# Attention on one core: the product of softmax weights and values issued as four matmuls of 32 queries

## The chip, the core and the metric

The kernel runs on one core of a Trainium2 chip. Its time is the device time of one execution, in microseconds (us). Five engines work side by side and meet through semaphores: TensorE (PE in the profile; its weight loads have a row of their own, PEld), VectorE (DVE), ScalarE (ACT), GpSimd (POOL) and SyncE (SP), which issues most of the DMA transfers. A matmul on TensorE has a stationary operand, which a weight load puts into the 128 x 128 array, and a moving operand, whose columns are streamed through it; the result goes to PSUM, one partition for each column of the stationary operand. Where an instruction uses 32 columns of the array only, the profile writes its shape as 128\*32 in place of 128\*128.

## The reference, cut to what matters

One layer of a hybrid decoder, for a prompt of 2048 tokens and a decode step of 8 samples. The part that the change touches is the dilated attention of the prompt: 6 heads of 64, each evaluated in three branches of (window, dilation).

```python
DILATED_BRANCHES = ((128, 1), (512, 4), (2048, 16))
...
def dilated_prompt(q, k, v, rel_bias, window, dil):
    ...                       # queries regrouped by residue mod dil, in blocks of 128
    s = jnp.einsum('bnqrhe,bnkrhe->bnrhqk', qb, kc).astype(jnp.float32) * scale + bias
    s = jnp.where(mask[None, :, None, None], s, NEG)
    lse = jax.nn.logsumexp(s, axis=-1)
    p = jnp.exp(s - lse[..., None]).astype(v.dtype)
    o = jnp.einsum('bnrhqk,bnkrhe->bnqrhe', p, vc).reshape(B, s_pad, H, E)[:, :S]
```

Each block of 128 queries meets its own block of 128 keys and, where there is one, the block before it. The second einsum, weights times values, is the product in question. Behind attention come an mLSTM mixer, an output projection and an MLP of width 4096, all in float32.

## The kernel before, in words

The work runs in stages: normalisation and the projections of the values; the projections of keys and queries; the projections of the mLSTM's inputs (`pmm` in the profile), the second half of them interleaved with attention; the mLSTM (`ppq`, `psA`, `up`, `nu`), interleaved with the rest of attention; the output projection; the MLP (`pf`), which takes the larger half of the time.

Attention is a generator. It goes through 6 heads, three branches and, in each branch, four groups of four blocks of 128 queries. Two blocks at a time go through three steps. `front` makes the scores: for each block two matmuls into the PSUM tile `ps_s` (L1073), then VectorE adds the bias and takes the row minimum (L1075), and ScalarE the exponential (`ex`, L1077). `turn` transposes the 128 x 128 pieces of `ex` on TensorE into `pt` (L1086), and VectorE copies them to SBUF as `pT` (L1088). `weigh` multiplies them by the values: for each block of queries and each of its one or two blocks of keys, one matmul with `pT` (128 keys x 128 queries) as the stationary operand and 65 columns of values and ones (`V`, 64 + 1) as the moving one, into a slice of the PSUM tile `po` (L1101). Two key blocks are added up in PSUM by the flags `start` and `stop`. After four blocks of queries ScalarE copies `po` to `R4` (L1103), and SyncE writes it to DRAM. There is one buffer of `po`; `ps_s` and `pt` share a pool that the other stages use too.

There are 450 such products: per head 16 in the branch with dilation 16 (one key block each), 28 in that with dilation 4 and 31 in that with dilation 1. All operands are float32, and each float32 matmul stands in the trace as two records of load and matmul, so that L1101 has 900 records.

The generators set the order in which instructions are written. A scheduler then orders them on each engine, by its own estimate of when each is ready; on TensorE it mixes the products with scores, transposes, projections and the mLSTM's matmuls. The instructions of one engine run in the order so fixed. In the mLSTM the state update has four matmuls of the form that the change uses (L441): 32 columns of the stationary operand each, written to 32 partitions each, with 161 moving columns.

Of the kernel before, what the change touches and what calls it, by code (L numbers as in the profile page):

```python
# [16 lines left out]
P = 128  # L17
# [42 lines left out]
def body(tc, I, O):  # L60
# [18 lines left out]
    pe = nc.tensor  # L79
# [959 lines left out]
    def attention(wk):  # L1039
# [54 lines left out]
        def weigh(tiles, pT, i, R4, dst):  # L1094
            if i == 0:
                acc_o[0] = ps.tile([P, 4, HD + 1], F32, name="po", tag="o", bufs=1)
            po = acc_o[0]
            for e, (_, w, _, vts) in enumerate(tiles):
                nk = w // P
                for kb in range(nk):  # L1100
                    pe.matmul(po[:, i + e], pT[:, e, kb], vts[kb], start=kb == 0, stop=kb == nk - 1)  # L1101
            if i:
                act.activation(R4[:, :, :HD + 1], po, AF.Copy)  # L1103
                nc.sync.dma_start(dst, R4)
# [4 lines left out]
        def flush():  # L1109
            if len(turned) == 1:  # L1110
                weigh(*turned.pop(0))
            if pend:
                tiles, ex, *rest = pend.pop(0)
                turned.append((tiles, turn(tiles, ex), *rest))
# [442 lines left out]
```

## Time and profile before

| what | value |
|---|---|
| time, median of 3 runs | 2720.37 us (2719.04 to 2722.34) |
| span of the profiled execution | 2721.4 us, 1.0 us above the median |
| TensorE busy | 2650.5 us, 97% of the span |
| VectorE, ScalarE busy | 1469.2 us (54%), 846.1 us (31%) |
| the products, L1101 | 900 records, first and last at 412.7 and 944.7 us |
| mean granted clock of TensorE | 0.983 |

The profiled execution's time is its span, from the first to the last instruction of the program. Busy shares are of that span. [...]

### The profile page before, as it was taken

Reading aid. Unit: us, or ns where it says so; the run is one execution under the profiler, and the core shown is the slowest. Engines: PE = TensorE matmul, PEld = TensorE weight load, DVE = VectorE, ACT = ScalarE, POOL = GpSimd, SP = SyncE. Lnnn points to the kernel's source line nnn. Section 1 sums busy time; section 2 is a strip of 40 time slices with the busy share of each in tenths; the row PEclk is TensorE's granted clock in tenths of the full one; section 3 lists DMA queues with packets and bytes.
Section 4 is the critical chain, followed back from the end, with each engine's and each line's share of the span. In section 5 each row is a group of like instructions: output and inputs, shape, how many; then the busy total and the mean of one; then the engine's idle time right before and its main releaser. Section 6 shows DMA issues by size and latency. Waiting matters only on the chain.

```text
span 2721.4 us, 39886 instructions
## 1 busy us (share of the span) xinstructions
PE 2650.5 (97%) x15366; PEld 2355.4 (87%) x15366; DVE 1469.2 (54%) x3444; ACT 846.1 (31%) x1898; POOL 202.7 (7%) x198
## 2 busy tenths in 40 slices
PE   8999999999999979999999999999999999999997
PEld 7999999999798867887888888888899999999996
DVE  6324655666477575753344444544754545454547
ACT  5321224444445443322321212121452121212123
POOL 1000000000344243110000000000000000000001
PEclk9999999999799979999999999999999999999998
DMA  8675566656476565543222312111241111111113
GB/s 196 152 196 163 167 171 142 152 140 159 129 185 169 145 189 159 174 152 125 70 97 66 101 63 62 46 55 40 93 155 55 39 55 39 55 40 55 40 38 119
DMA packets 334227, 302.57 MB, mean 111 GB/s; under 512 B 108543, under 2 KB 301467, under 8 KB 331092
## 3 DMA queue, kind: packets, MB, share of 16 engines
q1 hardware_dynamic: 332212, 296.39, 38.6%
q0 software_dynamic: 1536, 3.10, 0.5%
q8 instruction: 121, 1.98, 0.3%
q14 instruction: 70, 0.57, 0.1%
q10 hardware_dynamic: 288, 0.53, 0.1%
HBM read 220.94 MB, written 95.17 MB: 116 GB/s over the span
## 4 chain that ended last, share of the span: by engine, by line
PE 88%; DVE 4%; DMA 4%; ACT 2%; issue 1%; POOL 1%; SPq 0%; DVEq 0%; POOLq 0%; ACTq 0%
PE pf L163 19%; PE pf L162 19%; PE pf L164 19%; PE pmm L162 5%; PE pmm L164 5%; PE pmm L163 5%; PE ps_s L1073 4%; PE po L1101 3%; PE pt L1086 2%; PE ptp L176 1%; PE ppq L162 1%; PE up L437 1%; DMA tr_d<-tb_d 0%; PE ppq L164 0%; PE nu L458 0%
## 5 line engine op out<-in xcount | busy, mean ns | idle before, releaser
L1442 DVE TENSOR_TENSOR acc<-acc,pf 128x512 f32<-128x512 f32 (+2 forms) x600 | 343.1, 581 | 201.5 <-PE pf L164 200.2
L164 PE MATMUL pf<-rh,w2l 128*128 128x512 f32 (+2 forms) x1280 | 445.4, 348 | 0.0
L163 PE MATMUL pf<-rlo,w2h 128*128 128x512 f32 (+2 forms) x1280 | 445.0, 348 | 0.1
L162 PE MATMUL pf<-rh,w2h 128*128 128x512 f32 (+2 forms) x1280 | 444.4, 347 | 0.0
L162 PEld LDWEIGHTS pf<-rh,w2h 128*128 128x128 f32 x1280 | 241.8, 189 | 30.2 <-ACT rh L158 0.2
L163 PEld LDWEIGHTS pf<-rlo,w2h 128*128 128x128 f32 x1280 | 241.4, 189 | 30.6 <-DVE rlo L159 0.3
L164 PEld LDWEIGHTS pf<-rh,w2l 128*128 128x128 f32 x1280 | 241.3, 189 | 30.0 <-DVE w2l L159 0.2
L162 PE MATMUL pmm<-x,wh 128*128 128x344 f32 (+1 forms) x768 | 251.3, 327 | 0.0
L163 PE MATMUL pmm<-x,wh 128*128 128x344 f32 (+1 forms) x768 | 249.3, 325 | 0.0
L164 PE MATMUL pmm<-x,wl 128*128 128x344 f32 (+1 forms) x768 | 248.7, 324 | 0.0
L162 PE MATMUL pf<-h21h,w1h 128*128 128x512 f32 (+2 forms) x768 | 245.8, 320 | 0.0
L164 PE MATMUL pf<-h21h,w1l 128*128 128x512 f32 (+2 forms) x768 | 245.6, 320 | 0.0
L163 PE MATMUL pf<-h21l,w1h 128*128 128x512 f32 (+2 forms) x768 | 245.2, 319 | 0.0
L158 ACT ACTIVATE rh<-rl 128x264 fp32r<-128x264 f32 (+1 forms) x160 | 87.1, 545 | 465.9 <-PE pf L164 278.9
L163 PE MATMUL pf<-h20l,w1h 128*128 128x512 f32 x512 | 200.0, 391 | 0.0
L162 PE MATMUL pf<-h20h,w1h 128*128 128x512 f32 x512 | 199.9, 390 | 0.0
L164 PE MATMUL pf<-h20h,w1l 128*128 128x512 f32 x512 | 199.4, 390 | 0.0
L159 DVE TENSOR_TENSOR w1l<-w1r,w1h 128x1024 fp32r<-128x1024 f32 x64 | 78.4, 1225 | 184.7 <-ACT w1h L158 184.7
L1077 ACT ACTIVATE ex<-sm,R 128x256 f32<-128x256 f32 (+1 forms) x288 | 125.9, 457 | 145.4 <-DVE R L1075 140.9
L1421 DVE TENSOR_TENSOR rl<-rl 128x264 f32<-128x264 f32 (+1 forms) x160 | 93.2, 583 | 141.4 <-ACT rl L1420 141.4
L1075 DVE CUSTOM_DVE_ANT_0 sm<-ps_s,nb 128x256 f32<-128x256 f32 (+1 forms) x288 | 99.7, 362 | 118.4 <-PE ps_s L1073 88.9
L163 PEld LDWEIGHTS pf<-h21l,w1h 128*128 128x128 f32 x768 | 144.6, 188 | 12.8
(471 smaller groups left out, 5171.0 us busy)
## 6 DMA issues: line engine op xcount, KB each, us to landing
w1r<-in_w_ff_dram SPq DMA_DIRECT2D x64, 512.0 KB
w2r<-in_w_ff_dram SPq DMA_DIRECT2D x64, 512.0 KB
xt<-in_x_prompt_dram SPq DMA_DIRECT2D x31, 512.0 KB
xt<-x_d SPq DMA_DIRECT2D x25, 512.0 KB
R_d<-R SPq DMA_DIRECT2D x72, 132.0 KB
Rb<-R_d SPq DMA_DIRECT2D x48, 198.0 KB
V<-v_d SPq DMA_DIRECT2D x72, 130.0 KB
wraw<-in_w_in_dram SPq DMA_DIRECT2D x17, 512.0 KB
```

Source lines behind the costliest of these rows:

```text
L158: last_hi[0] = act.activation(hi, src, AF.Copy)
L159: last_lo[0] = (eng or vec).tensor_tensor(lo, src, hi.bitcast(F32), op=OP.subtract)
L162: pe.matmul(out, lh, rh, start=first, stop=False)
L163: pe.matmul(out, lh, rl, start=False, stop=False)
L164: pe.matmul(out, ll, rh, start=False, stop=last)
L1073: pe.matmul(out, Q[:, a:a + (P - 1) * d + 1:d], mv, start=i == 0, stop=i == 1)
L1075: vec.tensor_tensor_reduce(sm[:, :w], s_[:, e, c0:c0 + w], nb[:, o + bw - w:o + bw], 1.0, 3e38, OP.add, OP.min, mn)
L1077: act.activation(ex[:, e, :w], sm[:, :w], AF.Exp, bias=mn, scale=-1.0)
L1086: pe.transpose(pt[:, e, kb], ex[:, e, kb * P:(kb + 1) * P], ident)
L1101: pe.matmul(po[:, i + e], pT[:, e, kb], vts[kb], start=kb == 0, stop=kb == nk - 1)
L1421: vec.tensor_tensor(r[:, :n], r[:, :n], r[:, :n], op=OP.mult)
L1442: vec.tensor_tensor(av, av, pf[:, :n], op=OP.add)
```

## The change

Each product of 128 queries is written as four matmuls of 32 queries. The stationary operand of each is a quarter of the columns of `pT`, the moving operand is the whole of the same `vts[kb]` each time, and the result goes to 32 partitions of the same slice of `po`.

```diff
             for e, (_, w, _, vts) in enumerate(tiles):
                 nk = w // P
                 for kb in range(nk):
-                    pe.matmul(po[:, i + e], pT[:, e, kb], vts[kb], start=kb == 0, stop=kb == nk - 1)
+                    for c0 in range(0, P, 32):
+                        pe.matmul(po[c0:c0 + 32, i + e], pT[:, e, kb, c0:c0 + 32], vts[kb],
+                                  start=kb == 0, stop=kb == nk - 1)
             if i:
                 act.activation(R4[:, :, :HD + 1], po, AF.Copy)
                 nc.sync.dma_start(dst, R4)
```

The built program has 1800 matmuls of 32 x 65 (L1102) in place of 450 of 128 x 65 (L1101). The scheduler places instructions anew, and the order on TensorE differs from the first product on. In the order before, the 450 products stand in 165 unbroken runs; in the order now, the 1800 matmuls stand in 195 unbroken runs, 50 of them of 8 matmuls, 40 of 16, 39 of another length over 8, and 66 of under 8. Counting in each run how many matmuls fall on the quarter that is used most, the runs hold 499 rounds of up to four quarters, against 450 products.

At the start of attention, on TensorE, before (`po` is the product, `ps_s` the scores, `pt` the transposes, `pmm` a projection):

```order
L1086 MATMUL pt<-ident,ex 128x128
L1101 MATMUL po<-V,pT 128x65 x2
L1086 MATMUL pt<-ident,ex 128x128
L1073 MATMUL ps_s<-KH,Q_4213 128x256
L1073 MATMUL ps_s<-KL,Q_4213 128x256
L164 MATMUL pmm<-x_114,wl 128x344
```

and now, some rows later in the same place:

```order
L1086 MATMUL pt<-ident,ex 128x128 x3
L1102 MATMUL po<-V,pT 32x65 x5
L1073 MATMUL ps_s<-KH,Q_4213 128x256
L1073 MATMUL ps_s<-KL,Q_4213 128x256
L1102 MATMUL po<-V,pT 32x65 x3
L1073 MATMUL ps_s<-KH,Q_4213 128x256
```

Two products were one run of two; now the eight matmuls of two products can be cut into five and three, with scores of other blocks between them.

In the mLSTM stage, on TensorE, around the second state update (`up`), before:

```order
L1101 MATMUL po<-V,pT 128x65 x4
L1086 MATMUL pt<-ident,ex 128x128 x4
L437 MATMUL up<-v_7674,cw 128x161 x3
L439 MATMUL up<-v_7674,cw 128x161
L441 MATMUL up<-v_7674,cw 32x161 x4
L1101 MATMUL po<-V,pT 128x65 x4
```

and now:

```order
L1102 MATMUL po<-V,pT 32x65 x5
L418 MATMUL pt<-ident,cp 128x128
L1102 MATMUL po<-V,pT 32x65 x11
L1086 MATMUL pt<-ident,ex 128x128 x4
L437 MATMUL up<-v_8469,cw 128x161
L1073 MATMUL ps_s<-KH,Q_8256 128x256
L1073 MATMUL ps_s<-KL,Q_8256 128x256
L437 MATMUL up<-v_8469,cw 128x161 x2
L439 MATMUL up<-v_8469,cw 128x161
L441 MATMUL up<-v_8469,cw 32x161 x4
L1073 MATMUL ps_s<-KL,Q_8256 128x256
L1102 MATMUL po<-V,pT 32x65 x16
```

Here one run of four products became runs of 5 and 11 matmuls around a transpose, and the products behind the state update are parted from L441 by a score.

## The prediction

> **What bounds the kernel now.** I read the page first: busy shares, the 40 slices, and the chain that ended last.
>
> ```profile
> span 2721.4 us, 39886 instructions
> PE 2650.5 (97%) x15366; PEld 2355.4 (87%) x15366; DVE 1469.2 (54%) x3444; ACT 846.1 (31%) x1898; POOL 202.7 (7%) x198
> PE   8999999999999979999999999999999999999997
> PE 88%; DVE 4%; DMA 4%; ACT 2%; issue 1%; POOL 1%; SPq 0%; DVEq 0%; POOLq 0%; ACTq 0%
> ```
>
> TensorE is busy in every slice and carries 88% of the chain; nothing else holds more than 4%. But busy is an average over stages, so I cut the span where the products run: the columns are the stretch, its length, busy time and records of each engine, the granted clock, and the DMA.
>
> ```profile
> 412.73:656.66 243.93, 243.69 (x1612) 235.70 (x1611) 147.21 (x565) 102.66 (x244) 0.00 (x0) 1.00 0.64 147
> 656.66:944.71 288.05, 272.84 (x1855) 243.58 (x1855) 186.41 (x602) 136.93 (x406) 105.63 (x97) 0.93 0.60 158
> ```
>
> In the first stretch (attention beside projections) TensorE is never free: 243.69 of 243.93 us, at full clock. In the second (attention beside the mLSTM) it is free for 15.2 of 288.05 us. In both, a nanosecond that TensorE loses or gains moves the end, except for what those 15 us can take. VectorE and ScalarE have room (147 and 103 of 244 us). So the question is what a product costs TensorE, not who waits for it.
>
> A busy interval does not tell that, since intervals overlap. I read the order of time, where the distance between starts is the cost; one full run of four products, loads first, then matmuls:
>
> ```profile
> 507.96 0.97 PEld L1101 LDWEIGHTS po<-V,pT 128*128 128x128 f32 x8
> 508.85 0.31 PEld L1073 LDWEIGHTS ps_s<-KH,Q 128*128 128x128 f32 x1
> 507.96 0.27 PE L1086 MATMUL pt<-ident,ex 128*128 128x128 f32 x1
> 508.06 1.00 PE L1101 MATMUL po<-V,pT 128*128 128x65 f32 x8
> ```
>
> Eight loads take 508.85 - 507.96 = 0.89 us, 0.111 each, 0.2225 for a product (two records). The loads stand back to back: 65 moving columns stream faster than 128 columns of weights load, so the product is bound by its loads and the stream hides behind them. The first load also starts with the transpose's matmul before it (507.96 both): it hides behind that.
>
> **The change part by part.** The 450 products cost 450 x 0.2225 = 100.1 us now. They are replaced by 1800 matmuls on quarters of the array. The nearest row is L441, which has that form already: four quarters, two records each, but 161 moving columns.
>
> ```profile
> 784.09 1.01 PE L437 MATMUL up<-v,cw 128*128 128x161 f32 x6
> 784.94 0.44 PE L439 MATMUL up<-v,cw 128*128 128x161 f32 x2
> 785.31 0.48 PE L441 MATMUL up<-v,cw 128*32 128x161 f32 x8
> 785.72 0.60 PE L1073 MATMUL ps_s<-KL,Q 128*128 128x256 f32 x1
> 785.30 0.16 PEld L441 LDWEIGHTS up<-v,cw 128*32 128x32 f32 x8 [0.17 <-issue]
> 785.72 0.31 PEld L1073 LDWEIGHTS ps_s<-KL,Q 128*128 128x128 f32 x1 [0.25 <-issue]
> 785.08 0.30 PE L439 MATMUL up<-v,cw 128*128 128x161 f32 x1
> 785.47 0.32 PE L441 MATMUL up<-v,cw 128*32 128x161 f32 x4
> ```
>
> (The last two are the same records asked for alone: the second of L439, and the last four of L441.) Three things are read here.
>
> *The stream.* Six full-width records of L437 take 784.94 - 784.09 = 0.85 us, 0.14 each for 161 columns; 65 columns are then 0.14 x 65 / 161 = 0.0565 us.
>
> *The quarters run side by side.* All eight matmuls of L441 start within 0.18 us, in two waves 0.16 apart (785.31, 785.47): one wave streams on all four quarters at once, and the second follows when the first has streamed. Only the first load shows (0.16 against a stream of 0.14). So a product of four quarters should cost two waves, 2 x 0.0565 = 0.113 us instead of 0.2225: the bound moves from loads to stream, and the work itself is halved.
>
> *The change of form has a price at both ends.* The second full-width matmul started at 785.08 and streamed until 785.22; the first load of L441 starts at 785.30, 0.09 later, and the load engine shows it as 0.17 of idle with nothing that it waited for ("issue"). On the way back, from the first load at 785.30 to the next full-width load at 785.72 are 0.42 us, of which two waves are 0.28; some 0.13 to 0.14 (I take 0.13) remain for the first quarter's load, the quarters' stagger and the drain. No load crosses the border. In the old form the first load of a run hides behind the stream of the matmul before it, about 0.11 us for a transpose (a transpose was followed by the next start in 0.10 us above); now it waits for the end of that stream. A run thus costs 0.11 + 0.09 + 0.13 = 0.33 us on top of its waves.
>
> How many runs there are comes from the built order: 195 runs with 499 rounds of quarters (cut products cost an extra round). The sum:
>
> - runs: 195 x 0.33 = 64.4 us
> - rounds: 499 x 0.113 = 56.4 us
> - removed: 450 x 0.2225 = 100.1 us
> - difference: +20.7 us, slower.
>
> By stretch: until the last projection 103 runs, 265 rounds, 243 products, 34.0 + 29.9 - 54.1 = +9.8; in the mLSTM's stretch 92, 234 and 207, 30.4 + 26.4 - 46.1 = +10.7. A run pays for its two borders only above 0.33 / 0.11 = 3 products, and the average run holds 450 / 195 = 2.3.
>
> What is hidden: the added instructions themselves. L441 hands out eight loads and eight matmuls in 0.18 us, so 16 of them do not bound a round of 0.113 us by more than its own length; if they did, the price is under the first rival. ScalarE's copy of `po` and SyncE's write are unchanged, 72 each. Waiting behind a longer run are the scores, on which VectorE waits already (88.9 us in all at L1075, on the page's costliest groups), and it has 97 us free in the first stretch; it ends nothing.
>
> ```profile
> L1075 DVE CUSTOM_DVE_ANT_0 sm<-ps_s,nb 128x256 f32<-128x256 f32 (+1 forms) x288 | 99.7, 362 | 118.4 <-PE ps_s L1073 88.9
> ```
>
> Bounds. A round cannot fall below the stream, 0.113; at worst it costs what a product costs now, 0.2225, if the quarters' records block each other (+55 us more). A run costs at least nothing if it begins and ends in a wait that TensorE has anyway; in the second stretch 15.2 us of such waits could hide all +10.7, which leaves +10. I take the middle values, since L441 shows each of them in the same stage, at the same clock, on the same type.
>
> [...]
>
> **The rivals.**
>
> 1. *Quarters block each other in a longer run.* L441 is one round; a run here has two to four, and a quarter's next load must find its place free. The load of a quarter is 0.16 - 0.14 = 0.02 to 0.03 us; if it shows in each wave, 499 x 2 x 0.03 = +30, in all +51: 2772 us.
>
> 2. *The clock.* TensorE was granted half clock in parts of the second stretch:
>
> ```profile
> 678.60:682.00 3.40, 3.40 (x25) 2.35 (x26) 1.65 (x3) 1.48 (x5) 0.00 (x0) 1.00 1.04 291
> 682.00:695.70 13.70, 13.70 (x59) 10.61 (x60) 3.16 (x8) 3.45 (x12) 1.25 (x1) 0.50 0.49 139
> ```
>
> The 3.4 us before it have few records and many changes of form (25 in 3.40 us, at L224 and L225), and no idle. If the new borders call up two more such stretches, each loses half of 13.7 us: 20.7 + 13.7 = +34, 2755 us. Against it: outside the borders TensorE stays full, and the first stretch, the fullest, has clock 1.00. [...]
>
> 3. *The mLSTM's waits swallow their part.* Then +10 remains: 2730 us. For it, 15.2 us free in that stretch; against it, TensorE takes its instructions in order, and most runs do not stand beside a wait.
>
> 4. *Faster: the borders cost less than the rounds save.* The rounds alone save 100.1 - 56.4 = 43.7 us, so below 43.7 / 195 = 0.224 us a run the sign turns. If the two drains (0.09 each) did not show, a run would cost 0.15: 29.3 - 43.7 = -14, 2706 us. Nothing speaks for it but that only some switches were looked at; L441's idle of 0.17 and 0.25 speaks against.
>
> **How the numbers follow.** Forecast +20.7 on 2721.4, 2742 for a profiled execution; that one stood 1.0 us above the median, so 2741 us. Chances: forecast 0.66, rivals 0.12, 0.08, 0.08 and 0.06. The range: below, rival 3 and a little less, 2727; above, rival 1, 2775. A difference under 0.2% (5.4 us) cannot be told from none. Rival 4 gives nearly all of "faster", 0.05; its rest, the low end of rival 3 and of the forecast give 0.07 to "same"; slower has 0.88.
>
> **What would show it.** In the order of time, rounds of eight matmuls about 0.113 us apart inside a run, and an idle of 0.17 (into a run) and 0.25 (out of it) on the loads' row, put down to "issue". The first stretch grows from 243.9 to about 254 us, the second from 288 to about 299, everything before and after as it was. Wrong would be: rounds of 0.17 or more (rival 1); a mean clock below 0.93 in the second stretch (rival 2); a second stretch that does not grow (rival 3); or borders without idle (rival 4).

## The result and the profile after

The change makes the kernel slower: 2756.64 us median (2753.2 to 2763.85) against 2720.23, a ratio of 1.0134 with a 95% interval of 1.0116 to 1.0153. A second series gave 1.0139 (1.0124 to 1.0155). The forecast was 2741; the time lies inside the range, 16 us above the point, and the loss is 36 us where 20.7 was forecast.

The page of the changed kernel: span, engines, and TensorE's 40 slices.

```profile
span 2751.6 us, 45313 instructions
PE 2675.1 (97%) x18066; PEld 2326.9 (85%) x18066; DVE 1479.9 (54%) x3444; ACT 850.9 (31%) x1898; POOL 199.5 (7%) x198
PE   8999999999998988999999999999999999999998
```

2700 more matmul records (two for each of the 1350 added matmuls), less busy time on the loads, and TensorE as full as before. Busy shares say nothing about the loss; the stretches do. First the profiled execution of the change, then a second one; the columns are stretch, length, busy time and records of each engine, mean granted clock of TensorE, DMA. The rows are: up to the first product, attention beside projections, attention beside the mLSTM, and the mLSTM alone until the MLP.

```profile
0.00:418.61 418.61, 399.87 (x2498) 389.33 (x2498) 206.62 (x526) 138.87 (x312) 14.04 (x29) 0.98 0.63 171
418.61:671.79 253.18, 251.71 (x3070) 217.19 (x3070) 148.29 (x567) 103.44 (x244) 0.00 (x0) 1.00 0.61 142
671.79:965.96 294.17, 277.64 (x3094) 222.83 (x3092) 193.99 (x601) 139.26 (x405) 103.06 (x97) 0.95 0.60 155
965.96:1068.16 102.20, 83.70 (x511) 72.90 (x511) 62.39 (x161) 46.02 (x144) 36.72 (x34) 0.82 0.54 154
```

```profile
0.00:413.67 413.67, 395.34 (x2497) 384.56 (x2498) 206.61 (x526) 139.03 (x312) 13.99 (x29) 0.99 0.64 174
413.67:666.78 253.11, 251.75 (x3070) 217.13 (x3070) 148.31 (x567) 103.11 (x244) 0.00 (x0) 1.00 0.61 142
666.78:964.26 297.48, 282.79 (x3093) 228.04 (x3092) 192.47 (x601) 139.41 (x405) 103.27 (x97) 0.93 0.59 153
964.26:1067.19 102.93, 84.42 (x511) 73.30 (x511) 62.77 (x161) 45.94 (x144) 37.03 (x34) 0.80 0.54 153
```

The kernel before has also been profiled twice. Its first execution, cut at the same points of the program (the prediction cut some 0.3 us earlier):

```profile
0.00:412.73 412.73, 393.58 (x2497) 383.29 (x2498) 206.60 (x526) 139.02 (x312) 13.99 (x29) 0.99 0.66 174
412.73:656.98 244.25, 244.01 (x1613) 236.02 (x1612) 147.50 (x566) 102.66 (x244) 0.00 (x0) 1.00 0.64 147
656.98:944.99 288.01, 272.80 (x1856) 243.47 (x1854) 186.12 (x602) 136.93 (x406) 105.63 (x97) 0.93 0.60 158
944.99:1039.38 94.39, 78.15 (x507) 67.92 (x507) 59.81 (x161) 44.91 (x143) 38.14 (x34) 0.86 0.57 166
```

The second execution of the kernel before, all four:

```profile
0.00:412.34 412.34, 393.73 (x2498) 383.48 (x2498) 206.66 (x526) 138.37 (x312) 13.99 (x29) 0.99 0.64 174
412.34:656.46 244.12, 243.90 (x1613) 236.09 (x1612) 147.47 (x566) 102.68 (x244) 0.00 (x0) 1.00 0.62 147
656.46:942.33 285.87, 272.03 (x1855) 243.34 (x1854) 187.66 (x602) 137.24 (x406) 106.70 (x97) 0.93 0.60 159
942.33:1035.37 93.04, 76.34 (x507) 66.17 (x507) 60.50 (x161) 44.98 (x143) 38.68 (x34) 0.87 0.56 169
```

Two columns split each length into parts: length less PE busy is TensorE's free time, and (1 - clock) x length is what the lowered clock took. What is left I call work: TensorE's time at full clock. (The clock is printed to 0.01, so work is good to about 1.5 us in the long stretches.)

| stretch, means of two profiles | before | after | difference | of it work | free | clock |
|---|---|---|---|---|---|---|
| to the first product | 412.5 | 416.1 | +3.6 | | | |
| attention beside projections | 244.2 | 253.1 | +9.0 | +7.8 | +1.2 | 0 |
| attention beside the mLSTM | 286.9 | 295.8 | +8.9 | +10.1 | +1.1 | -2.3 |
| mLSTM alone | 93.7 | 102.6 | +8.9 | 0.0 | +2.0 | +6.9 |
| MLP | 1682.4 | 1684.1 | +1.7 | | | |
| span | 2719.8 | 2751.8 | +32.0 | | | |

For the mLSTM alone: 102.20 - 18.50 - 0.18 x 102.20 = 65.3 and 102.93 - 18.51 - 0.20 x 102.93 = 63.8 after, against 94.39 - 16.24 - 0.14 x 94.39 = 64.9 and 93.04 - 16.70 - 0.13 x 93.04 = 64.2 before. The work there is the same; the time is not.

The profiled executions of the change were on the fast side of theirs, and one of the kernel before on the slow side, so the table holds 32 of the 36 us. Every execution also lists its span and its mean clock. (1 - clock) x span, averaged, is 41 to 43 us for the kernel before (23, 15 and 17 executions in three series) and 55 us for the change (two sets of four). So some 13 to 14 of the 36 us went with a lower clock, and some 22 are left for everything else.

For the first row, the first profile of the change has half clock in places between 328 and 355 us and the second one has not, on a part of TensorE's order that the change leaves as it was:

```profile
328.20:355.50 27.30, 27.30 (x151) 27.30 (x151) 8.35 (x22) 2.81 (x6) 0.00 (x0) 0.75 0.49 129
328.20:355.50 27.30, 27.30 (x192) 27.30 (x192) 11.63 (x29) 4.21 (x8) 0.00 (x0) 1.00 0.54 148
```

Then one run of two products and one of four in the order of time, from the first profile of the change, loads first:

```profile
438.65 0.27 PEld L1102 LDWEIGHTS po<-V,pT 128*32 128x32 f32 x16 [0.25 <-issue]
439.02 0.31 PEld L1086 LDWEIGHTS pt<-ident,ex 128*128 128x128 f32 x3
440.56 0.50 PEld L1102 LDWEIGHTS po<-V,pT 128*32 128x32 f32 x32 [0.17 <-issue]
441.15 0.19 PEld L164 LDWEIGHTS pmm<-x,wl 128*128 128x128 f32 x1
440.25 0.38 PE L1086 MATMUL pt<-ident,ex 128*128 128x128 f32 x2
440.56 0.66 PE L1102 MATMUL po<-V,pT 128*32 128x65 f32 x32
```

A matmul record of L1102 lasts 0.22 us in the median and overlaps its neighbours, so distances between starts are read. From a run's first load to the next full-width load are 0.37 us for two rounds and 0.59 for four: (0.59 - 0.37) / 2 = 0.11 us a round and 0.37 - 2 x 0.114 = 0.14 of border behind it. Over all runs at full clock the medians are 0.25 us for one round, 0.366 for two and 0.593 for four, 0.114 a round. The border in front is the idle in brackets, put down to "issue". The prediction also named an idle of 0.25 us on the way out of a run; that did not show: 439.02 - 438.92 and 441.15 - 441.06 are 0.10 and 0.09, and the median over the 195 runs is 0.09. A run of four products, from the start of the transpose before it to the next load, has a median of 0.794 us, where it took 0.893 before; a run of two takes 0.575, where it took 0.410. (Taken to the start of the next matmul in place of the next load, a run of two takes 0.576, where it took 0.519: short runs lose 0.06 to 0.16 us, and the sum has 0.11.) Long runs gain, short ones lose, and short ones are the majority.

### The profile page after: what moved, and what is told of

The parts are those of the page before. It is cut to its first block, busy times and chain, and to the rows that moved or that the text cites. A ratio compares the mean times of both kernels' runs of the same rounds, so it can differ in the third digit from the quotient of the medians.

```text
span 2751.6 us, 45313 instructions
## 1 busy us (share of the span) xinstructions
PE 2675.1 (97%) x18066; PEld 2326.9 (85%) x18066; DVE 1479.9 (54%) x3444; ACT 850.9 (31%) x1898; POOL 199.5 (7%) x198
## 4 chain that ended last, share of the span: by engine, by line
PE 65%; DVE 4%; DMA 2%; ACT 1%; issue 1%; POOL 0%; SPq 0%; DVEq 0%; ACTq 0%
PE pf L163 19%; PE pf L162 19%; PE pf L164 19%; PE ps_s L1073 1%; PE ppq L162 1%; PE po L1102 1%; PE pt L1086 1%; PE ppq L164 1%; PE ppq L163 1%; PE ptp L176 0%; PE nu L458 0%; PE up L437 0%; PE nu L460 0%; PE nu L461 0%; DVE hden L464 0%
```

## The experiments

Theory A is that of the prediction: each run of quarters costs 0.33 us, each round 0.113, and a full-width product 0.2225; the rest of the loss is clock and idle time. Its rival B: a quarter matmul is dear by itself, wherever it stands. Times are compared with those of the kernel before in the same series (2718.87, 2718.55 and 2719.64 us); the ratios are those of the record and not the quotients of two medians. The last column is (1 - clock) x span, averaged over all executions; for the kernel before it is 42, 41 and 43 us in the three series.

| version | median us | ratio (95%) | beside projections | beside mLSTM: length, work | clock, all executions |
|---|---|---|---|---|---|
| before again | 2721.79 | 1.0011 (0.9997 to 1.0025) | 244.1 | 285.9, 252 | 44 |
| full width, unbroken runs | 2740.39 | 1.0076 (1.0049 to 1.0103) | 244.2 | 301.0, 255 | 54 |
| quarters, unbroken runs | 2743.75 | 1.0080 (1.0061 to 1.0100) | 246.7 | 302.3, 245 | 56 |
| full width, four blocks at once | 2752.16 | 1.0128 (1.0114 to 1.0142) | 244.5 | 313.6, 253 | 64 |
| quarters, four blocks at once | 2726.39 | 1.0023 (1.0011 to 1.0036) | 235.5 | 291.2, 241 | 57 |
| the same, loops swapped | 2730.64 | 1.0055 (1.0041 to 1.0068) | 237.9 | 290.9, 245 | 59 |
| the change again | 2754.20 | 1.0139 (1.0124 to 1.0155) | 253.1 | 297.5, 262 | 55 |
| the change, first three heads | 2734.78 | 1.0053 (1.0034 to 1.0072) | 252.0 | 297.6, 251 | 50 |
| the change, last three heads | 2739.03 | 1.0068 (1.0047 to 1.0090) | 245.5 | 296.2, 262 | 48 |
| halves of 64 | 2740.92 | 1.0078 (1.0053 to 1.0103) | 250.5 | 295.5, 252 | 52 |
| four blocks, first three heads | 2714.60 | 0.9991 (0.9975 to 1.0007) | 233.9 | 288.1, 254 | 47 |
| the same again | 2715.84 | 0.9983 (0.9969 to 0.9996) | 231.9 | 289.4, 253 | 50 |

### The kernel before against itself

No edit.

> The kernel before, run once more against itself. Theory A (the time outside the two stretches with products follows TensorE's granted clock, which falls to a half in other places from one execution to the next): the ratio is 1.000, but the profile shows half-clock stretches at places other than 160, 682 to 733, 815 to 897 and 969 to 1010 us, and stages without products move by up to some 6 us. Theory B (the 5.9 us before the first product and the 7.8 us behind the last one belong to the change): the stages of this run equal those of the first profile of before within 1 us.

The ratio is 1.0011, its interval holds 1. Its executions spread from 2717 to 2732 us. The stretches of the profile differ by at most 2.1 us, and half clock fell at other places (811.5 to 821.7 in place of 815.1 to 818.6 us; 965.1 to 975.3 in place of 968.7 to 989.2). So a few us in the stretches with the mLSTM are noise of the clock, as theory A has it. Differences of 9 us in both profiles of the change are more than that, though two profiles of one version, at the end of this section, still differ by 6 us behind attention. The change's second profile was this:

> The change once more, for a second profile of it. If the +5.9 us before the first product and the +7.8 us after the last one were a matter of where half clock fell: the stretch before the first product at 412 to 413 us, that of the products as in the first profile (253 and 294 us), the median near 2750 us. If they belong to the change: 418 and 102 us again.

One of each: the stretch before the first product came back to 413.7, the one behind attention stayed at 102.9. The first came and went with the clock from one execution of this program to the next. The second stands in both profiles of the change and in neither of the kernel before; it is no matter of the quarters as such, since the full-width version with four blocks at once, which has none, has 100.6 us and a clock of 0.80 there.

### Unbroken runs, in quarters and in full width

```diff
-            for e, (_, w, _, vts) in enumerate(tiles):
+            with tc.high_priority():
+                for e, (_, w, _, vts) in enumerate(tiles):
                 ...
```

in the change (143 runs, 450 rounds) and, as a control for the order, in the kernel before (148 runs).

> Quarters as in the change, with that precedence: 143 unbroken runs and 450 rounds for 195 and 499. Theory A (0.33 us a run, 0.113 us a round): 143 x 0.33 + 450 x 0.113 = 98.0 against 100.1 us, so 2 us below before, about 22 us below the change by the same sum. Theory B (each quarter matmul is dear by itself, the change's +36 us over its 1350 more matmuls): as slow as the change, +30 to +36 us.

> Full-width products as before, but given precedence in the scheduler, so that the products of a pair of blocks stand together: 148 runs for 165. A control for the order alone. Theory A (only runs and rounds of quarters have a price): within 4 us of before. Theory B (the new order itself costs): 5 us or more above before.

Both miss A as whole times. The control itself is some 21 us slower than before, so its theory B was met: a new order costs by itself, without a single quarter. No version holds the change's own order in full width, so what the order alone costs the change as a whole stays open. Where TensorE alone sets the pace, in the first stretch, the sum holds: full width 244.2 as before; quarters 246.7, of which 2.8 us are free time of TensorE, where 81 runs and 245 rounds give 26.7 + 27.7 - 245 x 0.2225 = -0.1. With the same quarters the change had 253.1. Rival B is out here: nearly as many quarter matmuls (980, and 972 in the change) cost 6.4 us less by standing in 81 runs instead of 103. In the mLSTM's stretch both are 14 to 15 us longer than before. By length, free time and clock (300.99, 18.70, 0.91 and 302.30, 27.25, 0.90), half clock has 7 us of the control's 14 and free time 4; with quarters half clock has 10, free time 13, and the work is 7 less. The edit puts products ahead of the mLSTM's own instructions there, but which of them came too late was not followed up.

### Four blocks at once, in quarters and in full width

```diff
             if i == 0:
-                acc_o[0] = ps.tile([P, 4, HD + 1], F32, name="po", tag="o", bufs=1)
-            po = acc_o[0]
-            for e, (_, w, _, vts) in enumerate(tiles):
+                acc_o[0] = (tiles, pT)
+                return
+            po = ps.tile([P, 4, HD + 1], F32, name="po", tag="o", bufs=1)
+            with tc.high_priority():
+                for i_, (tiles_, pT_) in ((2, (tiles, pT)), (0, acc_o[0])):
                 ...
```

The products of a pair of blocks wait for the second pair, and all but the first are pinned behind one another: 72 runs, 41 of them in the first stretch.

> Quarters, and the products of all four blocks of a group issued together: 72 unbroken runs and 450 rounds. Theory A: 72 x 0.33 + 450 x 0.113 = 74.6 against 100.1 us, 25 us below before, near 2695 us, unless the later transposes wait for the held weights. Theory B (dear by itself): +30 us or more.

> Full-width products, those of four blocks issued together, in the same order as the four-block quarters: the control that leaves the form alone as the difference between the two. Theory A (0.33 us a run and 0.113 us a round of quarters against 0.2225 us a product): the first stretch (attention beside projections) as before, 244 us, where the quarters had 235.5; the mLSTM's stretch longer than before through the order, as with the unbroken full-width runs (301 against 286 to 288 us); in all 2730 to 2740 us, above the four-block quarters. Theory B (quarters are dear by themselves): below the four-block quarters, at before's time.

The runs hold the same products in the same sequence, though not quite at the same places among the other instructions: quarters 2726.39, full width 2752.16 (in two series; ratios 1.0023 and 1.0128). The sign is the opposite of the change's, as A has it and B has not. The full-width version missed A's 2730 to 2740 by 12 us, and as a whole time the difference is not the form's alone: half clock took 64 us in the one and 57 in the other. The stretches are the better test. First the full width, then the quarters, beside projections and beside the mLSTM:

```profile
413.67:658.12 244.45, 244.24 (x1609) 235.01 (x1608) 148.00 (x561) 103.92 (x243) 0.00 (x0) 1.00 0.62 145
658.12:971.76 313.64, 293.65 (x1855) 257.12 (x1854) 189.04 (x602) 138.15 (x406) 104.55 (x97) 0.87 0.57 147
```

```profile
417.92:653.40 235.48, 233.04 (x3078) 212.12 (x3078) 147.47 (x561) 104.12 (x243) 0.00 (x0) 0.99 0.63 153
653.40:944.57 291.17, 264.76 (x3090) 224.56 (x3089) 192.46 (x602) 139.67 (x407) 104.75 (x97) 0.92 0.59 157
```

First stretch: the sum is 41 x 0.33 + 245 x 0.113 - 54.5 = -13.3 us. Measured is -9.0, with 2.2 us more free time and one half-clock stretch of 3.4 us, which took 1.7: -12.9 without them. In the second stretch the work falls by 11.4 us (241.5 against 252.9; the sum says 31 x 0.33 + 205 x 0.113 - 205 x 0.2225 = -12.2), but TensorE's free time is 26.4 us where it was 14 to 15, and the stretch is 4 us longer than before. There a gain in work turned into waiting and, by 3 us, into half clock. In the full-width version the loss is mostly the clock's: work as before, but clock 0.87 takes 41 us in place of 20. The quarters as a whole missed A's 2695 by 31 us: some 16 of them here, 4 in the first stretch, and about 5 each in the stretch before the first product (417.9) and in that behind attention (99.1).

### The order of the quarters

```diff
-                        for kb in range(nk):
-                            for c0 in range(0, P, 32):
+                        for c0 in range(0, P, 32):
+                            for kb in range(nk):
```

in the version with four blocks at once.

> The four-block quarters with the loops swapped: both key blocks of one quarter stand next to each other, where quarters rotated before. Same runs, same number of matmuls. If the array lets quarters run side by side whatever their order in the queue: the body of a run of 32 matmuls stays at 0.59 us for four rounds. If a quarter's second matmul blocks those behind it: a product pair takes up to four streams of 0.226 instead of two rounds of 0.113, and runs of 32 take 1.0 us or more; the whole some 20 to 40 us above the four-block quarters.

A run of eight products, quarters rotating, then swapped:

```profile
441.75 0.95 PEld L1106 LDWEIGHTS po<-V,pT 128*32 128x32 f32 x64 [0.17 <-issue]
442.79 0.31 PEld L1073 LDWEIGHTS ps_s<-KH,Q 128*128 128x128 f32 x1
```

```profile
444.62 1.02 PEld L1106 LDWEIGHTS po<-V,pT 128*32 128x32 f32 x64 [0.17 <-issue]
445.73 0.31 PEld L1073 LDWEIGHTS ps_s<-KH,Q 128*128 128x128 f32 x1
```

1.04 us against 1.11 for eight rounds: with 0.14 of border, 0.11 and 0.12 a round. (The expectation named runs of 32; it is the runs of 64 records that have two key blocks here.) Had a quarter's second matmul blocked those behind it, each pair of rounds would have taken up to four times 0.226 us. The quarters ran side by side in both orders, which also settles rival 1 of the prediction.

### The change for some heads only

```diff
-                    for c0 in range(0, P, 32):
+                    cw_ = 32 if calls[0] <= 72 else P
+                    for c0 in range(0, P, cw_):
```

(`calls` counts the calls of `weigh`; 72 are three heads; the other version has `> 72`.)

> The change for the first three heads alone, products as before for the rest. Theory A (runs and rounds): 94 runs, about 245 rounds for 225 products, 31.0 + 27.7 - 50.1 = +8.6 us, all in the first stretch (253 against 244); behind it as before, 2727 us in all. Theory D (what the change loses in the mLSTM's stretch and behind comes from what went before, a shift in time): these stretches longer too, 2735 us or more.

> The change for the last three heads alone. Theory A with what the two profiles of the change showed: first stretch 244 to 246; the mLSTM's stretch and the one behind it together 14 to 21 us above the 379 to 382 of before, of which the sum of runs and rounds explains 10.7 and TensorE's idle time and half clock the rest: 2735 to 2742 us. Theory D: 2730 us or less.

```profile
411.91:663.86 251.95, 250.52 (x2962) 218.67 (x2962) 147.61 (x566) 103.18 (x244) 0.00 (x0) 1.00 0.60 143
663.86:961.43 297.57, 280.89 (x1855) 249.30 (x1854) 191.63 (x602) 138.36 (x406) 106.96 (x97) 0.90 0.58 153
```

```profile
412.31:657.81 245.50, 245.27 (x1721) 234.51 (x1720) 147.66 (x566) 102.54 (x244) 0.00 (x0) 1.00 0.61 146
657.81:954.00 296.19, 282.29 (x3093) 228.08 (x3092) 193.62 (x602) 138.84 (x405) 102.93 (x97) 0.93 0.58 154
954.00:1056.10 102.10, 83.96 (x511) 73.65 (x511) 62.35 (x161) 45.94 (x144) 36.30 (x34) 0.82 0.53 154
```

Each part shows its own cost where it stands: +7.8 us in the first stretch for the first heads (8.6 expected; 1.2 of the 7.8 are free time), +1.3 there and +9 of work in the second for the last heads, and the 102 us behind attention come with the last heads alone (95.0 with the first; one profile each). The last heads' version is as A had it (2739.03, 2735 to 2742 expected). But the first heads' version also lost 10.6 us in the mLSTM's stretch, with work as before (251) and a clock of 0.90: A's "behind it as before" fell, and D's number, 2735, was met. D's cause, a shift in time, is not shown: the last version below shifts that stretch by 10 us the other way and leaves it as long as it was.

### Halves

```diff
-                    for c0 in range(0, P, 32):
-                        pe.matmul(po[c0:c0 + 32, i + e], pT[:, e, kb, c0:c0 + 32], vts[kb],
+                    for c0 in range(0, P, 64):
+                        pe.matmul(po[c0:c0 + 64, i + e], pT[:, e, kb, c0:c0 + 64], vts[kb],
```

> Two matmuls of 64 queries on halves of the array in place of four on quarters: 179 runs. If the price is the change of form at a run's borders and the gain two streams in place of two loads, halves do as quarters do: the first stretch 252 to 255 us, the whole within 8 us of the change. If the price goes with the number of matmuls (900 for 1800): half of the change's loss, the first stretch near 248 us.

The first stretch is 250.5, between the two figures, so this one doesn't decide; the change without its 1.5 us of free time there would be at 251.7. Single runs say more: 0.265 us from the first load to the next full-width load for one round, 0.383 for two and 0.616 for four, 0.117 a round and 0.15 of border. Half as many matmuls cost the same round and the same border, which is against a price for each matmul. The whole missed A's figure: it is 13 to 16 us below the change, and in the mLSTM's stretch its work came out at 252 us, without the 10 us that quarters added there. With 78 runs and 219 rounds there the sum would still have 78 x 0.35 + 219 x 0.117 - 207 x 0.2225 = +6.9 us, and in the first stretch, with 101 runs and 259 rounds, +11.6 where +6.3 was measured. So for halves the sum is 5 to 7 us too high in both; why, I can't say.

### A version that gains

The four-block quarters lost their gain in the mLSTM's stretch. So they were used for the first three heads alone, which fall beside the projections, and products as before for the other three.

> Quarters in unbroken runs of four blocks for the first three heads, which fall into the first stretch; products as before for the other three. Theory A: 36 x 0.33 + 225 x 0.113 - 225 x 0.2225 = -12.7 us in the first stretch, of which the four-block quarters showed two thirds (244.2 to 235.5), and the mLSTM's stretch as before: 2708 to 2712 us, below both kernels. Theory C (the mLSTM's stretch gets longer whenever the order before it changes): the first stretch shorter, but the whole within 5 us of before or above.

> The version with four-block quarters for the first three heads once more, for a closer figure: the first stretch at 234 us as in its first profile, the rest as before; a ratio of 0.996 to 0.999 to before.

```profile
413.86:647.77 233.91, 231.22 (x2954) 212.37 (x2954) 147.43 (x561) 103.50 (x242) 0.00 (x0) 1.00 0.64 153
647.77:935.83 288.06, 274.21 (x1855) 242.67 (x1854) 187.78 (x602) 136.88 (x406) 105.70 (x97) 0.93 0.60 158
```

The first stretch is 10.3 us shorter, and 12.2 in the second profile (12.7 by the sum); the mLSTM's is as before. The whole is 4 us shorter than before in both series, with one interval that holds 1 and one that does not (0.9969 to 0.9996). So it is the fastest of all, ahead of the kernel before by 0.1 to 0.2% at best. The first run missed A's 2708 to 2712 and lies inside C's 5 us; the second lies inside its own range (0.996 to 0.999). 6 to 8 us of what the first stretch gives do not arrive, and the clock has them: it took 47 and 50 us, where it took 41 and 43 in the kernel before of the same series. Without that part the two series stand 10 and 11 us below before. Its two profiles have spans of 2706.0 and 2714.3 us, and differ mainly behind attention (89.6 and 95.8 us, clock 0.90 and 0.84).

## Why the prediction was right, and where it was short

*The cost of a round* (0.113): right. 0.114 in the change, in runs of one to four rounds, and 0.11 in runs of eight products in the four-block version. The prediction's ground that 16 records handed out in 0.18 us would not bound a round was no proof, since 0.18 is longer than 0.113; the measured rounds show it. In the one round of L441 the eight loads had ended by 785.46, before the second wave of matmuls began at 785.47, so no load stood between the waves. Longer runs kept to that with their 0.114 us a round: with a load of 0.03 us exposed in each wave, as rival 1 has it, a round would have taken 2 x (0.0565 + 0.03) = 0.17. That a quarter's next load has to wait until its place is free, the ground of that rival, no run shows. Rival 1 is out.

*The border of a run* (0.33): right. Measured 0.14 behind a run, and 0.20 in front of it after a transpose; after scores 0.21 to 0.32, since these stream longer (two scores start 0.25 us apart in the trace). In the old form a run after scores was longer too (0.515 against 0.410 for two products), so the sum held. The rows of L441 put the step from the end of the stream before it to its first load at 0.09 us; how the 0.14 on the way back is made up of load, stagger and drain was the author's estimate, and no run takes it apart. Rival 4 is out.

*The sum by stretch*: +9.8 and +10.7 forecast; +9.0 measured in the first (7.8 of it work), +10.1 of work in the second. Its waits did not swallow it (free time rose by 1.1 us), so rival 3 is out. Over all executions, what is left without the clock's part rose by some 22 us, against +20.7; in the table above it is 17.9 of work and 4.3 of free time.

*"Everything before and after as it was"*, and with it a clock that stays as it was: wrong, and the step that failed. The mLSTM alone, behind attention, took 8.9 us more for the same work, 6.9 by half clock and 2.0 idle, and over all executions half clock took 13 to 14 us more. Rival 2 priced just that (13.7 us, 2755 in all; measured 2756.6), but looked for it in the second stretch, whose clock did not fall in the mean, and put it down to the new borders. That cause is not shown: behind attention no product is left, and the full-width versions lost about as much clock or more (54 and 64 us in the table, the change 55). Its chance, 0.08, was too small. I had reasoned that outside the borders TensorE stays full, and read the clock as a matter of the stretch where products are, when the profile before already had 0.86 behind it. That 2756.6 lies inside the range is luck in part: the top of the range was set for rival 1, which did not happen.

What makes the clock fall can be narrowed from the traces, though no experiment tested it. In (1 - clock) x length, the mLSTM's stretch lost 20 and 20 us in two executions of the kernel before, 15 and 21 in two of the change, 20 and 26 in two of the gaining version, 30 with quarters for the first heads alone, which that stretch does not hold, and 41 with four full-width blocks at once. Up to the MLP, half clock comes in pieces of 3.41 us on a fixed grid in all fourteen traces, and the grid lies differently against the program from one execution to the next (in the two of the kernel before, half clock began at 815.1 and 811.5 us, 3.6 apart and so 0.2 off the grid). The traces hold 3907 pieces of this grid at full clock. Where fewer than 1500 moving columns were streamed in one (all matmul records that start in it, each counted), the next piece was at half clock in 75 of 81 cases; with 3000 or more, in 26 of 3468. A busy TensorE need not stream many columns: in the 3.41 us ahead of the half clock at 682 us in the first profile of the kernel before it was busy throughout and streamed 1600, and ahead of that at 328 us in the first profile of the change busy throughout with 2446. In the latter piece stand rows like these, two columns each.

```profile
324.97 0.36 PE L591 MATMUL pso<-WT,ky 97*128 97x2 f32 x2
325.19 0.36 PE L591 MATMUL pso<-WT,kx 128*128 128x2 f32 x2
```

So part of the loss varies from one execution of a program to the next (15 and 21 us in two of the change), and part goes with the order that the scheduler makes (41 us with four full-width blocks at once, 20 before). That the first part follows the place of the grid is the author's reading and was not shown. Every new order tried here lost more clock than that of the kernel before (47 to 64 us of all executions, against 41 to 44); which of its instructions make the thin pieces was not found.

## What to carry to other kernels

Splitting a matmul by columns of the stationary operand paid here, where the load bound it: the quarters loaded and streamed side by side, and a product's cost fell from 0.2225 to 0.114 us. It was paid for once per unbroken run, with 0.33 us in the sum, so look at the built order and count runs before counting matmuls; here the sum puts the turn at three products a run (245 products in 81 runs came out even). A gain on TensorE arrived where TensorE alone set the pace (9.0 us of 13.3 with four blocks at once), and turned mostly into idle time in the mLSTM's stretch (11.4 us less work, and 26.4 us free where it was 14 to 15). Full-width versions in a new order lost 54 and 64 us to the clock, the kernel before 41 to 43, so compare the clock of all executions too, with a control in the old form.

## What the runs showed of the hardware

- The four quarters do not need to alternate in the queue: eight rounds took 1.04 us in rotation and 1.11 us with both key blocks of one quarter back to back.
- Halves and quarters have the same price: 0.117 and 0.114 us a round, 0.15 and 0.14 us behind a run.
- TensorE's granted clock fell to a half at different places in two executions of one program, once on a part that had full clock in the other (0.75 and 1.00 between 328 and 355 us), with no idle time of TensorE there; two profiles of one version differed by 8 us.
- Half clock followed pieces of 3.41 us in which TensorE streamed few columns: 75 of 81 with fewer than 1500 columns, 26 of 3468 with 3000 or more. It also followed pieces with TensorE busy throughout and 1600 or 2446 columns.
